# The down projection's seven products in another form, with the weights' sums made on chip ahead of their use

## The chip, the cores and the metric

The kernel runs on one core of a Trainium2 chip. The metric is the device time of one execution in microseconds (us), lower is better; the figure for a kernel is the median of several runs. Beside it stands one profiled execution, whose span runs from its first to its last instruction. The engines are named as the profile names them: PE multiplies matrices (PEld is its weight load), DVE, ACT and POOL (GpSimd) work on tiles, SP only issues transfers.

## What is computed

One step of a hybrid decoder layer over 1032 tokens (1024 of a prompt, 8 of a second group):

```python
hn = rmsnorm(x, norm1_w)
...
x = x + jnp.concatenate([y_ssd, y_pool], axis=-1) @ w_out
hn = rmsnorm(x, norm2_w)
...
u, ffn_new = causal_dwconv(u, ffn_buf, ffn_conv_w, ffn_conv_b)
...
x = x + (jax.nn.silu(gate) * val) @ w_down
```

and a last RMS norm. The first product with `w_out` is the output projection; the last, with the 2816 x 1024 matrix `w_down`, the down projection. Everything is in float32.

## The kernel before, in words

**Arithmetic.** A float32 product is made of three matmuls in a reduced format: each operand is split into a high part (an ACT copy) and a low part (a DVE subtraction of the high part from the value), and high x high, high x low and low x high are added up in PSUM. `split` (L207) does this for moving operands, `weight_parts` (L132 to 142) for weights. Weights come from DRAM into a `raw` tile (a pool of four) or an `s` tile (a pool of seven), and their two parts lie in one `wop` tile (a pool of four). So each transfer of weights waits for the split of an earlier block, and each split for PE to be done with an earlier `wop`.

**Stages.** After the state-space and pooling parts comes the output projection (`w_out`, L896): its operands `yh`, `yl` are split six at a time, and each of the eight output tiles takes 6 + 6 + 4 of them. Beside it `down_sums` (L1240) makes sums of blocks of `w_down` for later: twelve calls, each with four SP loads, four GpSimd additions or subtractions (L1253) and four GpSimd stores to DRAM scratch (L1255). Then the up projection runs over 22 pairs of 128-wide tiles of the feed-forward width (`up_pair`); `up_close` (L1184) does the convolution, SiLU and gate, and `spill` (L1226) writes what the down projection will need to DRAM scratch `td`: for each two tiles of the width, seven rows of 128 x 516, one row for each of seven products.

**The down projection** (`down`, L1305) is one 2 x 2 step of fast matrix multiplication: the width is cut into even and odd tiles (11 each), the tokens into halves of 516, the outputs into four pairs of tiles. Seven block products take the place of eight. For each product, `down_ops` (L1262) loads eleven 128 x 516 operands from `td` through GpSimd's queue (L1270, `g<-td`) and splits them; `down_weights` (L1277) loads 12 weight pieces (four output pairs m by three groups of 4, 4 and 3 width tiles); `piece` (L1291) issues 18 or 24 matmuls of 128 x 258 for a piece, the two quarters of tokens one after the other; and a `sink` adds the result into `x2`, the running sum of the layer, or, in before, into `u`. In all 7 x 264 = 1848 matmuls. The order of products before is p1, p2, p5, p6, p7, p4, p3. In p1, p2 and p4 the weights are single blocks of `w_down`; the other four read their sums back from scratch (`s<-sd`). The first product runs its pieces over all four m for one group of width tiles before the next group, in all eight PSUM banks; the others finish an m before they start the next. Squares for the last norm are made by ACT and added up by GpSimd (L1367) as blocks of `x2` are finished, and `norm_half` (L1459) writes the first half of the tokens out.

**What sets the order.** The code states what depends on what. The order of the instructions on each engine is fixed when the kernel is built, by a scheduler that goes by its own estimate of when each could start; at run time each engine takes its instructions strictly in that order and waits at each for what it needs. Issuing a transfer on GpSimd's queue is such an instruction: a transfer stands behind any addition written before it.

Of the kernel before, what the change touches and what calls it, by code (L numbers as in the profile page):

```python
# [75 lines left out]
class Kernel:  # L76
# [817 lines left out]
    def w_out(self, pf):  # L894
# [12 lines left out]
        self.sums = {}  # L907
        todo = [(m, s) for s in range(len(PIECES)) for m in range(KT // 2)]

        def part(ops, k0, first, done=None):  # L910
            for n in range(KT):
                if first <= n < first + 6:
                    self.down_sums(len(todo), *todo.pop(0))
# [9 lines left out]
                if done is not None:  # L923
                    done(n)

        part(ops, 0, 0)
# [5 lines left out]
        part(ops, 6, 1)  # L932
# [251 lines left out]
    def up_close(self, j, us):  # L1184
# [4 lines left out]
        if j == FT - 1:  # L1189
            self.begun = self.down_ops("p1", 0, 4)  # L1190
            high = self.high
# [32 lines left out]
    def spill(self, x, y, s, t):  # L1224


        nc = self.nc
        a, b = slice(0, TH), slice(TH, TOK)
        td = self.dram.tile([7, P, TH], F32, name=self.nm("td"))
        self.td.append(td)  # L1230
        rows = lambda r, n: td[r : r + n].rearrange("s p c -> p s c")
        halves = lambda t: t[:, :TOK].rearrange("p (s c) -> p s c", s=2)
        for out, in0, in1 in (
            (s[:, a], x[:, b], x[:, a]), (s[:, b], y[:, b], x[:, b]),
            (t[:, a], y[:, b], s[:, a]), (t[:, b], y[:, a], t[:, a]),
        ):
            nc.vector.tensor_tensor(out=out, in0=in0, in1=in1, op=ALU.subtract)
        self.puts += [(td[0], x[:, a]), (rows(1, 2), halves(y)), (rows(3, 2), halves(s)), (rows(5, 2), halves(t))]

    def down_sums(self, i, m, s):  # L1240

        nc, d = self.nc, self.d
        k0, nk = PIECES[s]
        w = nk * P
        mk = lambda tag, bufs=1: self.ph.tile([P, 2, 512], F32, tag=tag, name=self.nm("ds"), bufs=bufs)
        x, y, z = mk("v", 2), mk(("mh", "ml")[i % 2]), mk(("sa", "sb")[i % 2])
        blk = {"11": x[:, 0, :w], "12": x[:, 1, :w], "21": y[:, 0, :w], "22": y[:, 1, :w]}
        for k, r, e in (("21", 1, 0), ("22", 1, 1), ("11", 0, 0), ("12", 0, 1)):
            o = (e * DK + k0) * P
            nc.sync.dma_start(blk[k], d["wdn"][2 * m + r][:, o : o + w])  # L1250

        def mix(p, out, in0, in1, op):
            nc.gpsimd.tensor_tensor(out=out, in0=in0, in1=in1, op=op)  # L1253
            self.sums[p, m, s] = self.dram.tile([P, w], F32, name=self.nm("sd"))
            nc.gpsimd.dma_start(self.sums[p, m, s], out)  # L1255

        s2 = z[:, 0, :w]
        mix("p5", blk["22"], blk["21"], blk["22"], ALU.add)
        mix("p7", blk["21"], blk["11"], blk["21"], ALU.subtract)
        mix("p6", s2, blk["22"], blk["11"], ALU.subtract)  # L1260
        mix("p3", blk["12"], blk["12"], s2, ALU.subtract)
# [15 lines left out]
    def down_weights(self, p, m, s, pool=None):  # L1277

        k0, nk = PIECES[s]
        w = nk * P  # L1280
        if p in DIRECT:
            i, e = DIRECT[p]
            o = (e * DK + k0) * P
            src = self.d["wdn"][2 * m + i][:, o : o + w]
        else:
            src = self.sums[p, m, s]
        raw = self.raw(p not in DIRECT)[:, :w]
        self.nc.sync.dma_start(raw, src)
        return self.weight_parts(raw, w, self.nc.vector, pool)

    def piece(self, out, both, ops, s, q):  # L1291

        nc = self.nc
        k0, nk = PIECES[s]
        part = slice(q * TQ, (q + 1) * TQ)
        for i in range(nk):
            wh, wl = both[:, i * P : (i + 1) * P], both[:, 512 + i * P : 512 + (i + 1) * P]
            xh, xl = (t[:, part] for t in ops[k0 + i])
            for j, (a, b) in enumerate(((wh, xh), (wh, xl), (wl, xh))):
                self.pe = nc.tensor.matmul(  # L1300
                    out, a, b, start=(s == 0 and i == 0 and j == 0),
                    stop=(s == len(PIECES) - 1 and i == nk - 1 and j == 2),
                ).ins

    def down(self, ops):  # L1305
# [19 lines left out]
        us = [self.big.tile([P, 2, TH], F32, tag="big", name=self.nm("U")) for _ in range(2)]  # L1325

        def sink(p, m, q, ps):
            part = slice(q * TQ, (q + 1) * TQ)
            u = us[m // 2][:, m % 2, part]
            block = lambda i, t: x2[2 * m + i][:, half(t)][:, part]  # L1330

            def add(eng, out, in1):
                eng.tensor_tensor(out=out, in0=out, in1=in1, op=ALU.add)  # L1333

            if p == "p1":
                nc.scalar.activation(u, ps, AF.Copy)  # L1336
            elif p == "p2":
                add(nc.vector, block(0, 0), u)
                add(nc.vector, block(0, 0), ps)
            elif p == "p5":  # L1340
                add(nc.vector, block(0, 1), ps)
                add(nc.vector, block(1, 1), ps)
# [270 lines left out]
```

## Time and profile before

| | |
|---|---|
| median of 3 runs | 1409.72 us |
| lowest, highest | 1406.89, 1411.45 us |
| the profiled execution | 1407.76 us |
| its span | 1406.0 us |
| mean granted clock of PE in it | 0.984 |

An instruction's row gives its engine, the line of the kernel, the operation, the tile that it writes and those that it reads, their shapes and how many instructions the row holds. A group's row gives the busy time of all and the mean of one in ns, then the idle time just before them on their engine and what ended most of it. A row of the timeline starts with its start and length. The granted clock of a window is 1.00 when PE has its full clock.

### The profile page before, as it was taken

The page shows a single profiled execution, that of the slowest core. Times are in us where ns is not written, and L with a number is a line of the kernel's source. Part 1 is how long each engine was busy: PE and PEld are TensorE (multiplying, and loading weights), DVE is VectorE, ACT ScalarE, POOL GpSimd, SP SyncE. Part 2 cuts the span into 40 slices and gives each one's busy share as a digit, 9 for nine tenths or more (in the row PEclk, how much of TensorE's full clock was granted, in tenths as well). Part 3 has the DMA queues.
Part 4 walks back from the last instruction along what each step waited for, and adds up shares of the span by engine and source line. Part 5 has one row for each costly group of instructions (what it writes and reads, how often), then busy time and mean ns, then how long its engine had stood idle before and what let it go on. Part 6 is the DMA issues. An engine that isn't in the chain of part 4 may idle for free. (4 is left out here: it accounts for less than half of the span.)

```text
span 1406.0 us, 26779 instructions
## 1 busy us (share of the span) xinstructions
PE 1360.4 (97%) x10360; PEld 1312.9 (93%) x10360; DVE 991.2 (70%) x1453; ACT 700.6 (50%) x1408; POOL 561.5 (40%) x704
## 2 busy tenths in 40 slices
PE   8999999979999999999979999999999999999997
PEld 7799879968799999899979999999999999999997
DVE  6575898669865684844689877777776787567743
ACT  6346774546644451311456545554554465444452
POOL 4233465888668305774222212212222224214122
PEclk9999999989999999999999999999999999999999
DMA  6031235243331256675477877777777769657513
GB/s 248 1 108 38 93 118 168 81 142 116 94 104 62 74 192 209 214 253 178 152 204 148 210 205 193 187 207 183 185 187 201 196 207 328 225 185 235 180 55 121
DMA packets 117820, 228.09 MB, mean 162 GB/s; under 512 B 19884, under 2 KB 37116, under 8 KB 117692
## 3 DMA queue, kind: packets, MB, share of 16 engines
q1 hardware_dynamic: 73772, 130.21, 29.3%
q0 software_dynamic: 27056, 70.22, 19.8%
q10 hardware_dynamic: 16864, 25.95, 5.6%
q8 instruction: 81, 1.33, 0.4%
q14 instruction: 47, 0.39, 0.1%
HBM read 169.64 MB, written 45.15 MB: 153 GB/s over the span
## 5 line engine op out<-in xcount | busy, mean ns | idle before, releaser
L1118 PE MATMUL g<-op,wop 128*128 128x258 f32 x3696 | 446.9, 283 | 4.3 <-DVE op L1048 1.6
L1118 PEld LDWEIGHTS g<-op,wop 128*128 128x128 f32 x3696 | 445.3, 189 | 5.6 <-DVE op L1048 2.0
L140 ACT ACTIVATE wop<-raw 128x512 fp32r<-128x512 f32 (+1 forms) x208 | 125.9, 608 | 231.2 <-PE g L161 139.7
L1300 PE MATMUL g<-op,wop 128*128 128x258 f32 x1848 | 224.9, 283 | 1.6 <-ACT op L210 0.9
L159 PE MATMUL g<-hh,wop 128*128 128x344 f32 x696 | 226.1, 325 | 0.0
L160 PE MATMUL g<-hl,wop 128*128 128x344 f32 x696 | 225.3, 324 | 0.0
L1300 PEld LDWEIGHTS g<-op,wop 128*128 128x128 f32 x1848 | 222.5, 189 | 2.7 <-ACT op L210 1.1
L161 PE MATMUL g<-hh,wop 128*128 128x344 f32 x696 | 224.8, 323 | 0.0
L141 DVE TENSOR_TENSOR wop<-raw,wop 128x512 fp32r<-128x512 f32 (+1 forms) x186 | 159.7, 862 | 83.3 <-ACT wop L140 81.5
L140 ACT ACTIVATE wop<-s 128x512 fp32r<-128x512 f32 (+1 forms) x136 | 83.6, 620 | 137.6 <-PE g L1300 51.9
L1098 POOL DMA_DIRECT2D s<-s x44 | 37.7, 857 | 249.8 <-DVE wop L141 89.2
L159 PEld LDWEIGHTS g<-hh,wop 128*128 128x128 f32 x696 | 132.2, 190 | 1.2 <-issue 1.1
L161 PEld LDWEIGHTS g<-hh,wop 128*128 128x128 f32 x696 | 132.1, 190 | 1.2 <-issue 1.2
L160 PEld LDWEIGHTS g<-hl,wop 128*128 128x128 f32 x696 | 132.1, 190 | 0.5 <-issue 0.4
L1200 DVE SCALAR_TENSOR_TENSOR acc<-u,cst,acc 128x1048 f32<-128x1048 f32 x88 | 115.2, 1309 | 12.2 <-ACT acc L1198 10.6
L141 DVE TENSOR_TENSOR wop<-s,wop 128x512 fp32r<-128x512 f32 (+1 forms) x136 | 92.1, 682 | 36.5 <-ACT wop L140 34.1
L1178 DVE TENSOR_TENSOR u<-u,g 128x258 f32<-128x258 f32 (+2 forms) x176 | 58.0, 354 | 72.2 <-PE g L1118 67.6
L1175 ACT ACTIVATE u<-g 128x258 f32<-128x258 f32 (+2 forms) x220 | 69.6, 340 | 71.2 <-PE g L1118 71.2
L160 PE MATMUL g<-yl,wop 128*128 128x344 f32 x288 | 93.4, 325 | 3.2 <-DVE yl L211 3.2
L161 PE MATMUL g<-yh,wop 128*128 128x344 f32 x288 | 93.0, 323 | 0.0
L159 PE MATMUL g<-yh,wop 128*128 128x344 f32 x288 | 92.9, 323 | 0.0
L1270 POOL DMA_DIRECT2D g<-td x77 | 41.2, 539 | 123.1 <-DVE op L211 70.2
(276 smaller groups left out, 2333.9 us busy)
## 6 DMA issues: line engine op xcount, KB each, us to landing
s<-wup SPq DMA_DIRECT2D x88, 256.0 KB, 3.2
g<-td POOLq DMA_DIRECT2D x77, 258.0 KB, 4.5
raw<-wup SPq DMA_DIRECT2D x66, 256.0 KB, 4.1
raw<-win SPq DMA_DIRECT2D x58, 256.0 KB, 2.7
mix<-acd SPq DMA_DIRECT2D x16, 768.0 KB, 4.5
td<-acc ACTq DMA_DIRECT2D x22, 516.0 KB, 6.1
s<-wup POOLq DMA_DIRECT2D x44, 256.0 KB, 5.3
s<-s POOLq DMA_DIRECT2D x44, 256.0 KB, 3.9
```

The lines of the kernel that those rows point to most:

```text
L140: self.nc.scalar.activation(hi, raw[:, :w], AF.Copy)
L141: lo_eng.tensor_tensor(out=lo, in0=raw[:, :w], in1=hi.bitcast(F32), op=ALU.subtract)
L159: nc.tensor.matmul(ps[:, :n], wh, xh[:, sl], start=(first and k == 0), stop=False)
L160: nc.tensor.matmul(ps[:, :n], wh, xl[:, sl], start=False, stop=False)
L161: nc.tensor.matmul(ps[:, :n], wl, xh[:, sl], start=False, stop=(final and k == last))
L1098: nc.gpsimd.dma_start(t, raw[acc] if acc in raw else w[acc][j], accum_op=ALU.add)
L1118: nc.tensor.matmul(out, a, b, start=(p in OPENS and j == 1), stop=(j == 12), skip_group_check=True)
L1175: a = nc.scalar.activation(out, ps[:, s], AF.Copy, scale=-1.0 if p in ("p5", "p4") else 1.0)
L1178: nc.vector.tensor_tensor(out=out, in0=out, in1=ps[:, s], op=op)
L1200: nc.vector.scalar_tensor_tensor(out=acc, in0=u[:, k : k + FW], scalar=self.c("fw", 3 * n + k), in1=acc, op0=ALU.mult, op1=ALU.add)
L1270: self.loaded = self.nc.gpsimd.dma_start(st[:, j], self.td[i + j][ROW[p]]).ins
L1300: self.pe = nc.tensor.matmul(out, a, b, start=(s == 0 and i == 0 and j == 0), stop=(s == len(PIECES) - 1 and i == nk - 1 and j == 2),).ins
```

## The change

The seven products take another form. Their names are now n1 to n7, in the order n4, n2, n1, n5, n7, n3, n6. Two of them (n4, n3) use single blocks of `w_down`; the other five use a sum or difference of two blocks. Nothing of that is made ahead: `down_weights` loads the one block into an `s` tile and the other into a `raw` tile, and GpSimd adds them in the `s` tile before the split. That is 60 additions (40 of 128 x 512, 20 of 128 x 384) and 60 more loads than a single block would take. `down_sums` is gone, and with it everything beside the output projection. `spill` makes five sums for each two tiles rather than four, and the row of `td` that n4 reads is written first. Results go straight from PSUM into one or two blocks of `x2` (`into`), 96 additions of 128 x 258 rather than 88, with no copy to `u`. The 16 half tiles of `x2` are loaded 8 in n4, 4 in n2 and 4 in n1 (before: 4 in p1, 12 in p2). Squares are made in n2, n7, n3 and n6; `norm_half` for the first half moves from the last product into n3. In the last product the even and odd outputs change places.

```diff
-DOWN = ("p1", "p2", "p5", "p6", "p7", "p4", "p3")
-DIRECT = {"p1": (0, 0), "p2": (0, 1), "p4": (1, 1)}
-ROW = {"p1": 0, "p2": 1, "p3": 2, "p5": 3, "p7": 4, "p6": 5, "p4": 6}
+DOWN = ("n4", "n2", "n1", "n5", "n7", "n3", "n6")
+ROW = {"n2": 0, "n7": 1, "n5": 2, "n3": 3, "n6": 4, "n4": 5, "n1": 6}
+SRC = {
+    "n1": ((0, 0), (1, 1), ALU.subtract), "n2": ((1, 0), (1, 1), ALU.add), "n3": ((0, 0), None, None),
+    "n4": ((1, 1), None, None), "n5": ((0, 0), (0, 1), ALU.add), "n6": ((1, 0), (0, 0), ALU.add),
+    "n7": ((0, 1), (1, 1), ALU.add),
+}
+INTO = {
+    "n1": ((0, 0, ALU.add), (1, 1, ALU.subtract)), "n2": ((1, 0, ALU.add), (1, 1, ALU.subtract)),
+    "n3": ((0, 1, ALU.add), (1, 1, ALU.subtract)), "n4": ((1, 0, ALU.add), (0, 0, ALU.subtract)),
+    "n5": ((0, 0, ALU.subtract), (0, 1, ALU.add)), "n6": ((1, 1, ALU.add),), "n7": ((0, 0, ALU.add),),
+}
...
-                if first <= n < first + 6:
-                    self.down_sums(len(todo), *todo.pop(0))
...
-        for out, in0, in1 in (
-            (s[:, a], x[:, b], x[:, a]), (s[:, b], y[:, b], x[:, b]),
-            (t[:, a], y[:, b], s[:, a]), (t[:, b], y[:, a], t[:, a]),
+        for out, in0, in1, op in (
+            (t[:, a], y[:, a], x[:, a], ALU.subtract), (t[:, b], x[:, a], y[:, b], ALU.add),
+            (s[:, a], x[:, b], y[:, b], ALU.subtract), (s[:, b], x[:, a], x[:, b], ALU.add),
+            (y[:, a], y[:, a], y[:, b], ALU.add),
         ):
...
-        self.puts += [(td[0], x[:, a]), (rows(1, 2), halves(y)), (rows(3, 2), halves(s)), (rows(5, 2), halves(t))]
+        self.puts += [(rows(5, 2), halves(t)), (td[0], x[:, a]), (rows(3, 2), halves(s)), (rows(1, 2), halves(y))]
...
-        raw = self.raw(p not in DIRECT)[:, :w]
-        self.nc.sync.dma_start(raw, src)
-        return self.weight_parts(raw, w, self.nc.vector, pool)
+        one, two, op = SRC[p]
+        raw = self.raw(two is not None)[:, :w]
+        nc.sync.dma_start(raw, block(*one))
+        if two is not None:
+            more = self.raw(False)[:, :w]
+            nc.sync.dma_start(more, block(*two))
+            nc.gpsimd.tensor_tensor(out=raw, in0=raw, in1=more, op=op)
+        return self.weight_parts(raw, w, nc.vector, pool)
...
+    def into(self, x2, p, m, q, ps):
+
+        ins = None
+        for i, t, op in INTO[p]:
+            out = x2[2 * m + i][:, t * TH + q * TQ : t * TH + (q + 1) * TQ]
+            ins = self.nc.vector.tensor_tensor(out=out, in0=out, in1=ps, op=op).ins
+        return ins
...
-        ops += self.down_ops("p1", len(ops), DK - 1)
-        second = self.down_ops("p2", 0, 8)
-        ops += self.down_ops("p1", DK - 1)
+        ops += self.down_ops("n4", len(ops), DK - 1)
+        second = self.down_ops("n2", 0, 8)
+        ops += self.down_ops("n4", DK - 1)
...
+        whole = {"n2": (1, 0), "n7": (0, 0), "n3": (0, 1)}
...
-                load_x2([(n, 0) for n in range(0, KT, 2)])
+                load_x2([(n, 0) for n in range(KT)])
...
+                if p in whole:
+                    i, t = whole[p]
+                    square(2 * m + i, t)
+                if p == "n3" and m == 1:
+                    with self.behind(self.pe):
+                        self.norm_half(x2, 0, ssq[0], r_of(0))
```

The order of GpSimd's instructions at the end of the first product, before. Rows of `g` load operands two to a tile: here six of p2's and then p1's last one, `g_13225`; the `x` row loads half a tile of `x2`.

```order
L1270 DMA g_13198<-td_8997 128x516
L1270 DMA g_13198<-td_9514 128x516
L1270 DMA g_13207<-td_10031 128x516
L1270 DMA g_13207<-td_10548 128x516
L1270 DMA g_13216<-td_11065 128x516
L1270 DMA g_13216<-td_11582 128x516
L1270 DMA g_13225<-td_13151 128x516
L1322 DMA x_13234<-x2d 128x516
```

The same place now; `g_13008` is n4's last operand, the `s` rows are sums of n2's weights, each of an `s` tile and a `raw` tile.

```order
L1271 TENSOR_TENSOR s_13399<-s_13399,raw_13401 128x512
L1271 TENSOR_TENSOR s_13431<-s_13431,raw_13433 128x512
L1271 TENSOR_TENSOR s_13463<-s_13463,raw_13465 128x384
L1252 DMA g_12990<-td_9807 128x516
L1252 DMA g_12990<-td_10325 128x516
L1271 TENSOR_TENSOR s_13496<-s_13496,raw_13498 128x512
L1271 TENSOR_TENSOR s_13528<-s_13528,raw_13530 128x512
L1271 TENSOR_TENSOR s_13560<-s_13560,raw_13562 128x384
L1271 TENSOR_TENSOR s_13595<-s_13595,raw_13597 128x512
L1252 DMA g_12999<-td_10843 128x516
L1252 DMA g_12999<-td_11361 128x516
L1252 DMA g_13008<-td_12933 128x516
```

Seven sums now stand between the operand loads and ahead of the first product's last one.

SP's queue at the same place, before: the last four weight pieces of p1, then the first four of p2.

```order
L1288 DMA raw_13482<-wdn 128x384
L1288 DMA raw_13507<-wdn 128x384
L1288 DMA raw_13532<-wdn 128x384
L1288 DMA raw_13557<-wdn 128x384
L1288 DMA raw_13614<-wdn 128x512
L1288 DMA raw_13643<-wdn 128x512
L1288 DMA raw_13672<-wdn 128x384
L1288 DMA raw_13701<-wdn 128x512
```

And now: the last four pieces of n4 (L1267), then second blocks for n2's sums (L1270), whose first blocks have been issued earlier.

```order
L1267 DMA raw_13271<-wdn 128x384
L1267 DMA raw_13298<-wdn 128x384
L1267 DMA raw_13325<-wdn 128x384
L1267 DMA raw_13352<-wdn 128x384
L1270 DMA raw_13401<-wdn 128x512
L1270 DMA raw_13433<-wdn 128x512
L1270 DMA raw_13465<-wdn 128x384
L1270 DMA raw_13498<-wdn 128x512
```

The tiles `raw_13401` and on take the buffers of the pieces above them, as p2's blocks did before, and GpSimd's sums now read them.

GpSimd's queue in the third product, before: the operand loads of p5 in one run, its last one `g_14005`.

```order
L1270 DMA g_13978<-td_10031 128x516
L1270 DMA g_13978<-td_10548 128x516
L1270 DMA g_13987<-td_11065 128x516
L1270 DMA g_13987<-td_11582 128x516
L1270 DMA g_13996<-td_12099 128x516
L1270 DMA g_13996<-td_12616 128x516
L1270 DMA g_14005<-td_13151 128x516
```

And now, those of n1, its last one `g_13836`; the `ssq` row adds up squares of n2's results, `s_14281` is a sum for the next product.

```order
L1328 TENSOR_TENSOR ssq_13013<-ssq_13013,sq_13788 128x516
L1271 TENSOR_TENSOR s_14167<-s_14167,raw_14169 128x512
L1252 DMA g_13818<-td_10843 128x516
L1252 DMA g_13818<-td_11361 128x516
L1271 TENSOR_TENSOR s_14199<-s_14199,raw_14201 128x384
L1271 TENSOR_TENSOR s_14281<-s_14281,raw_14283 128x512
L1252 DMA g_13827<-td_11879 128x516
L1252 DMA g_13827<-td_12397 128x516
L1252 DMA g_13836<-td_12933 128x516
```

Sums of n1's own weights and of n5's first piece now lie between n1's operand loads.

More of the change, by code (lines that the diff above doesn't have):

```diff
@@ L905, in w_out, with part @@
             self.x2.append(t)
-        self.sums = {}
-        todo = [(m, s) for s in range(len(PIECES)) for m in range(KT // 2)]
-        def part(ops, k0, first, done=None):
+        def part(ops, k0):
             for n in range(KT):
-                if first <= n < first + 6:
-                    self.down_sums(len(todo), *todo.pop(0))
                 nk = len(ops)
@@ L922, in part @@
                 (self.gemm_k if n == KT - 1 else self.gemm)(ws, ops, evac)
-                if done is not None:
-                    done(n)
-        part(ops, 0, 0)
+        part(ops, 0)
         ops = []
@@ L931, in w_out @@
             ops.append(o)
-        part(ops, 6, 1)
+        part(ops, 6)
         ops = []
@@ L1324, in down @@
         half = lambda t: slice(t * TH, (t + 1) * TH)
[L1325 to L1342, printed above, removed]
-            elif p == "p6":
-                add(nc.vector, u, ps)
-                add(nc.vector, block(0, 1), u)
-            elif p == "p7":
-                add(nc.vector, u, ps)
-                add(nc.vector, block(1, 1), u)
-            elif p == "p4":
-                add(nc.vector, block(1, 0), u)
-                add(nc.vector, block(1, 0), ps)
-            else:
-                add(nc.vector, block(0, 1), ps)
+        cut = lambda ops, s: ops[PIECES[s][0] : PIECES[s][0] + PIECES[s][1]]
         mksq = lambda: self.ph.tile([P, TH], F32, tag="sq", name=self.nm("sq"), bufs=2)
@@ L1434, in down @@
                     ones()
-                if q == 0 and m == 1:
-                    with self.behind(self.pe):
-                        self.norm_half(x2, 0, ssq[0], r_of(0))
             ones()
```

89 lines of the change are left out of this document (31 added, 58 removed).

## The prediction

> **What bounds the kernel now.** I began with the page: span, engine shares, slices; then the chain of waits for the down projection; then windows over the stages that the change touches.
>
> ```profile
> span 1406.0 us, 26779 instructions
> PE 1360.4 (97%) x10360; PEld 1312.9 (93%) x10360; DVE 991.2 (70%) x1453; ACT 700.6 (50%) x1408; POOL 561.5 (40%) x704
> 1170.50 27.88 PE g L1300 x233
> ...
> 1200.34 6.10 DMA raw<-wdn
> ...
> 1207.75 155.47 PE g L1300 x1297
> ```
>
> PE is busy for 97%. In the down projection the chain is one run of 1297 matmuls, 155.47/1297 = 0.120 us each, behind one wait for a weight block, so a product of 264 matmuls takes 31.7 us. Both kernels do 7 x 264 = 1848 of them, so only what makes PE wait or run slow counts. The windows (length; busy time and instructions of PE, weight load, DVE, ACT, POOL; granted clock; DMA share; GB/s) show where it does:
>
> ```profile
> 560.00:580.00 20.00, 20.00 (x129) 20.00 (x128) 14.81 (x13) 4.05 (x7) 15.35 (x17) 1.00 0.82 273
> 580.00:600.00 20.00, 16.82 (x89) 16.09 (x88) 19.90 (x15) 7.97 (x10) 14.46 (x14) 0.83 0.55 170
> 585.00:590.00 5.00, 2.40 (x16) 2.12 (x14) 5.00 (x1) 0.97 (x2) 4.98 (x6) 0.96 0.37 138
> 590.00:595.00 5.00, 4.41 (x14) 3.97 (x15) 5.00 (x8) 3.38 (x4) 0.09 (x1) 0.50 0.80 249
> 595.00:600.00 5.00, 5.00 (x29) 5.00 (x28) 5.00 (x5) 0.53 (x1) 4.39 (x4) 0.85 0.59 135
> 1200.00:1210.00 10.00, 9.10 (x75) 8.85 (x74) 7.06 (x15) 5.42 (x13) 2.14 (x4) 1.00 0.93 346
> 1210.00:1360.00 150.00, 150.00 (x1256) 150.00 (x1255) 98.55 (x185) 70.75 (x128) 34.51 (x53) 1.00 0.52 166
> 1360.00:1370.00 10.00, 9.27 (x70) 8.68 (x70) 5.96 (x11) 7.07 (x16) 2.55 (x2) 1.00 0.19 62
> ```
>
> From 1210 to 1360 PE never idles, DVE has 98.55 of 150 us and GpSimd 34.51. The output projection loses time at 585 to 595, and there GpSimd is adding.
>
> **The change, part by part.** *A, the output projection.* Rows of the timelines of DVE, GpSimd and PE (start, length, instruction):
>
> ```profile
> 578.19 11.96 DVE L211 TENSOR_TENSOR yl<-xs,yh 128x1032 fp32r<-128x1032 f32 x4
> 590.54 1.22 DVE L211 TENSOR_TENSOR yl<-xs,yh 128x1032 fp32r<-128x1032 f32 x1
> 579.17 4.54 POOL L1253 TENSOR_TENSOR ds<-ds,ds 128x512 f32<-128x512 f32 x2
> 537.30 0.51 DVE L920 TENSOR_TENSOR x<-x,g 128x344 f32<-128x344 f32 x1 [0.57 <-PE g L161]
> 590.21 0.66 PE L160 MATMUL g<-yl,wop 128*128 128x344 f32 x1 [2.80 <-DVE yl L211]
> ```
>
> One subtraction alone takes 1.22 us; four beside GpSimd's adds (two of them at 579.17) take 11.96 instead of 4.9. PE waits 2.80 us for the last, then runs at a clock of 0.50. The window from 580 holds 89 matmuls and the one before it 129, 0.155 us each, so 40 are missing: 40 x 0.155 = 6.2 us. The change takes the adds away: **-6.2** (-6.2 to 0: zero if the split is late for another reason).
>
> *B, the first product's last operand.* The groups and transfers that price the new work (count, busy time, mean ns; a transfer's last figure is us from issue to landing):
>
> ```profile
> L1253 POOL TENSOR_TENSOR ds<-ds,ds 128x512 f32<-128x512 f32 x24 | 33.3, 1409 | 3.0 <-DMA ds<-wdn 2.8
> L1253 POOL TENSOR_TENSOR ds<-ds,ds 128x384 f32<-128x384 f32 x12 | 12.4, 1043 | 3.9 <-DMA ds<-wdn 3.8
> L1270 POOL DMA_DIRECT2D g<-td x77 | 41.2, 539 | 123.1 <-DVE op L211 70.2 <-PE g L1300 20.6 <-PE g L1118 13.2
> L210 ACT ACTIVATE op<-g 128x516 fp32r<-128x516 f32 x77 | 45.6, 622 | 3.3 <-DMA g<-td 2.1 <-DVE acc L1237 1.0
> g<-td POOLq DMA_DIRECT2D x77, 258.0 KB, 4.5
> raw<-wdn SPq DMA_DIRECT2D x24, 256.0 KB, 4.4
> s<-sd SPq DMA_DIRECT2D x32, 256.0 KB, 2.9
> raw<-wdn SPq DMA_DIRECT2D x8, 256.0 KB, 6.0
> x<-x2d POOLq DMA_DIRECT2D x16, 258.0 KB, 7.4
> ```
>
> The last two are of 1165 to 1205 alone. Before, the first product's last operand load leaves at 1172.44; it needs only an early tile. Now GpSimd's row of n4's last operand stands behind seven sums of n2 and four operand loads. The sums need second blocks, which SP loads into the four `raw` tiles, and those come free only as n4's pieces 9 to 12 are split. Before, the same tiles came free for p2's first four loads at these times:
>
> ```profile
> 1172.44 0.54 POOL L1270 DMA_DIRECT2D g<-td  x1 [5.86 <-DVE wop L141]
> 1187.33 0.87 SPq L1288 DMA_DIRECT2D raw<-wdn  x2
> 1189.83 0.33 SPq L1288 DMA_DIRECT2D raw<-wdn  x1
> 1192.68 0.33 SPq L1288 DMA_DIRECT2D raw<-wdn  x1
> ```
>
> With 4.4 us to land, sum 1 starts at 1191.8 and sums 1 to 3 end at 1193.2, 1194.6, 1195.7; two operand loads go until 1196.8. Sum 4 waits for the block of 1192.68, lands 1197.1, ends 1198.5. Sums 5 to 7 use the tiles that sums 1 to 3 freed, end at 1199.9, 1200.9, 1202.4. Two loads more, then the last operand's leaves at 1203.5, lands 4.5 later at 1208.0, and its high part is there 0.62 later: 1208.7. PE's order puts the 24 matmuls that use it at n4's end; p1's ended at 1198.39 by the chain, so PE is dry at 1198.39 - 24 x 0.12 = 1195.5. Wait: **+13.2** (9.9 with 2.9 to land, 16.8 with 6.0). Behind it on GpSimd stand n4's eight loads of x2, without which its sums can't leave PSUM: first issues 1204.1 and 1204.7, 7.4 to land, 1212.1, against n4's end at 1208.7 + 2.9: **+1** (0 to 4).
>
> *C, the clock after that wait.* By the rows above 2.80 us of idling were followed by a clock of 0.50 for about 6 us, a loss of 3.0: **+3.0** (0 to 3). The Trainium skill, "TensorE: Matmul & The Clock Gate", Part 1, has the clock halved after an idle window of about 3.4 us and back after about as long of activity. The first the row contradicts (2.80 us did it); by the second a wait costs about 1.7, and the sum would be 1.6 lower over this wait and D's.
>
> *D, n1.* Between n2's last operand and n1's last, GpSimd has 14 sums, 3 adds of squares and 15 loads, some 30 us for a product of 31.7, and it is tied to PE. n1's k8 load stands behind a sum of n5 whose `s` tile comes free when n1's sixth piece is split, for which PE must be 48 matmuls (5.8 us) into n1. Then, by the rows above and below, split 0.63 + 0.70, load of a block 2.9, sum 1.41, issue 0.54, landing 4.5, high part 0.62: 17.1 us after n1's start. PE gets to k8 after 96 matmuls, 11.5 us, and is 5.6 us early. k6, behind a sum whose tile n2's end frees, is there at about 13 and wanted after 72 matmuls, 8.6: 4.4 of the 5.6 fall there, 1.2 at k8. One add of squares in between (1.3) makes it **+7** (4 with 2.9 to land and no squares; 13 with the block landing in 6.0 and the operand in 7.4), and a second wait's clock **+2** (0 to 3).
>
> *E, n2, n5, n7, n6.* In n5 the k10 load stands behind a sum of n7; by steps like D's the operand is there 17.3 us into the product, wanted after 141 matmuls, 16.9. The last loads of n2, n7 and n6 stand behind sums in the same way. I choose about 1 each: **+4** (0 to 16, each wait like D's 4.4 at k6, less a little).
>
> *F.* Two gaps of before, 0.90 us at 1200 to 1210 and 0.73 at 1360 to 1370, need not come back: **-1** (-1.6 to 0).
>
> *At no cost.* Eleven more spill additions, one for each pair of up-projection tiles, like these:
>
> ```profile
> L1237 DVE TENSOR_TENSOR u<-acc,u 128x516 f32<-128x516 f32 x11 | 7.6, 690 | 0.0
> ```
>
> They run on DVE beside PE's matmuls of the up stage (7.6 us if that cover were gone). Eight more DVE adds of 0.42 into x2, hidden while DVE has a third free, 3.4 otherwise. Sixty more SP loads, 0.33 of issue each; their 40 x 256 + 20 x 192 KB over the 220 us of the projection are 64 GB/s, beside 166 at a DMA share of 0.52. The ACT copies of p1's results go, off the path. The norm of the first half moves a product earlier and runs beside matmuls either way.
>
> **Sum.** -6.2 + 13.2 + 1 + 3 + 7 + 2 + 4 - 1 = +23.0. On the profiled execution's 1407.8 us that is 1430.8. The median of the runs, 1409.7, lies 2.0 above it: **1433 us**. The lower ends give 1416, the upper 1466.
>
> **Rivals.**
>
> *Lock bound, 1424.* GpSimd's adds and DVE's operations on two operands in SBUF exclude each other:
>
> ```profile
> L211 DVE TENSOR_TENSOR op<-g,op 128x516 fp32r<-128x516 f32 x77 | 53.9, 721 | 3.0 <-ACT op L210 2.9
> L141 DVE TENSOR_TENSOR wop<-s,wop 128x512 fp32r<-128x512 f32 x120 | 83.6, 699 | 23.2 <-ACT wop L140 20.8
> L141 DVE TENSOR_TENSOR wop<-s,wop 128x384 fp32r<-128x384 f32 x16 | 8.9, 554 | 13.3 <-ACT wop L140 13.3
> L140 ACT ACTIVATE wop<-s 128x512 fp32r<-128x512 f32 x120 | 75.6, 633 | 117.5 <-PE g L1118 49.1 <-issue 36.2 <-PE g L1300 32.2
> L1333 DVE TENSOR_TENSOR x<-x,g 128x258 f32<-128x258 f32 x40 | 15.8, 419 | 23.7 <-PE g L1300 23.7
> L1367 POOL TENSOR_TENSOR ssq<-ssq,sq 128x516 f32<-128x516 f32 x10 | 13.2, 1331 | 32.3 <-ACT sq L1366 25.6 <-ACT ssq L1363 6.5
> ```
>
> A product takes DVE 11 x 0.721 + 8 x 0.699 + 4 x 0.554 = 15.7, and GpSimd's sums 8 x 1.409 + 4 x 1.043 = 15.4: 31.1 of 31.7 if exclusive. In n2 and n7, 4 x 1.331 of squares make it 36.4, 4.7 over each. If operand loads are not held otherwise: 1407.8 - 6.2 - 1 + 9.4 + 2 = 1412; where the adds from PSUM cannot overlap either (16 x 0.42 = 6.7, half in n7 and n6), up to 1437. Middle 1424. For it: A's 11.96 us. Against its upper end: the PSUM add at 537.30 took 0.51 beside an add of GpSimd. The Trainium skill, "SBUF — State Buffer", "SBUF: two separate sides", states this as a lock on a port pair that the two engines share, for the whole instruction; 11.96 us for four agrees. Chance 0.12.
>
> *Cascade, 1456.* Each sum waits for a `raw` tile, each tile for an earlier sum, and GpSimd's row is in order, so lateness in n1 is handed on: n2, n5 and n7 lose 6.5 each instead of 3 of E's 4 together (+16.5), and two more waits are long enough to halve the clock (+6): 1433 + 22.5. It decides if GpSimd's 30 us of work per product can't start before the product. Chance 0.20.
>
> *Faster, 1402.* The other side: n4's last operand leaves 13.2 us sooner than I have it, by 1190.3, because the `raw` tiles come free earlier than before's; no later wait opens. Then only A and F stay: 1407.8 + 2.0 - 6.2 - 1.6. Against it: the times above are set by PE's pace through pieces 5 to 8, which the change leaves. Chance 0.06.
>
> *The output projection doesn't gain, 1439.* The split could be late because its inputs are. The four subtractions ran end to end with GpSimd's adds, so I give this 0.06, inside my forecast's range.
>
> **How the numbers follow.** Forecast 0.52 beside the last rival's 0.06, which lies within 1420 to 1445 too; lock bound 0.12, cascade 0.20, faster 0.06; 0.04 stays for sums that cancel to within 0.3%, 4.2 us, about what a measurement here tells from no change. Faster 0.06, same 0.04, slower 0.90. The range runs from the lock rival's lower end, taken as 1413, to just above the cascade, 1460; outside lie the faster case, most of the same and the cascade's upper third.
>
> **What would show it.** Right: DVE's four yl subtractions at about 4.9 us and no clock of 0.50 near 590; a wait of PE of some 13 us for n4's last operand with GpSimd's adds of line 1271 ahead of its load; a shorter pair of waits about 8 to 12 us into n1; half clock behind each. Wrong: no PE wait at n4's end (then B, C fall, and it is near 1413 or below); waits of PE on DVE's splits rather than on operand loads (lock); waits above 4 us in n5 and n7 (cascade).

## The result and the profile after

The changed kernel takes 1453.7 us (median of 4 runs, 1450.7 to 1456.3), the kernel before beside it 1408.3: a ratio of 1.0323, 95% interval 1.0285 to 1.0362, or 45 us more. The forecast of 1433 was 21 us short; the range, 1413 to 1460, holds it.

The page of the changed kernel has these first lines:

```profile
span 1449.8 us, 26760 instructions
PE 1370.5 (95%) x10360; PEld 1318.3 (91%) x10360; DVE 1010.8 (70%) x1472; ACT 700.6 (48%) x1400; POOL 552.1 (38%) x668
```

PE does the same matmuls and now idles 79 us, before 46. Of the 44 us that the span grew, 34 are idle time of PE; the other 10 are the same matmuls taking longer, at a mean granted clock of 0.976 instead of 0.984. No other engine has come near to its limit, and GpSimd is, over the whole span, even less busy than before. So it is waiting, and a lower clock, and not work, that has been added. The windows of the changed kernel at the places that the prediction named (columns as before):

```profile
580.00:600.00 20.00, 20.00 (x129) 20.00 (x129) 12.52 (x19) 6.02 (x9) 0.00 (x0) 1.00 0.16 46
1198.00:1205.00 7.00, 6.66 (x37) 6.66 (x38) 5.12 (x13) 2.72 (x5) 1.65 (x4) 0.62 0.88 331
1210.00:1350.00 140.00, 125.93 (x994) 122.84 (x993) 102.76 (x141) 53.29 (x95) 84.20 (x95) 0.96 0.73 241
```

The output projection now does 129 matmuls from 580 to 600 at full clock, and DVE's four subtractions take 4.94 us instead of 11.96:

```profile
574.52 4.94 DVE L222 TENSOR_TENSOR yl<-xs,yh 128x1032 fp32r<-128x1032 f32 x4
```

From 1210 to 1350 PE loses 14 us, where the kernel before lost none from 1210 to 1360. Where PE waits is read from its timeline; the last bracket gives the wait and what ended it:

```profile
1160.82 26.78 PE L1283 MATMUL g<-op,wop 128*128 128x258 f32 x223
1198.34 37.36 PE L1283 MATMUL g<-op,wop 128*128 128x258 f32 x292 [10.75 <-ACT op L221]
...
1253.49 28.49 PE L1283 MATMUL g<-op,wop 128*128 128x258 f32 x219 [4.41 <-ACT op L221]
...
1382.10 7.44 PE L1283 MATMUL g<-op,wop 128*128 128x258 f32 x60 [2.44 <-DVE wop L152]
1395.18 4.54 PE L1283 MATMUL g<-op,wop 128*128 128x258 f32 x18 [5.64 <-ACT wop L151]
1404.02 0.58 PE L1283 MATMUL g<-op,wop 128*128 128x258 f32 x1 [4.30 <-ACT op L221]
...
1407.86 4.59 PE L1283 MATMUL g<-op,wop 128*128 128x258 f32 x21 [1.94 <-ACT wop L151]
```

The trace also gives the length of each product: the matmuls of the down projection are counted by their single records, and a product ends where each 264th ends. This table has the lengths in us, for the two kernels and for experiments told below. The first product is counted from the projection's first matmul.

| kernel | 1st | 2nd | 3rd | 4th | 5th | 6th | 7th | all |
|---|---|---|---|---|---|---|---|---|
| before | 34.6 | 32.9 | 31.5 | 31.6 | 31.6 | 31.6 | 36.7 | 230.6 |
| changed | 47.7 | 31.6 | 43.5 | 37.7 | 35.0 | 35.3 | 52.4 | 283.2 |
| no sums (e1) | 34.5 | 32.5 | 31.7 | 31.5 | 31.6 | 32.9 | 40.8 | 235.5 |
| narrow sums (e2) | 47.3 | 31.7 | 37.5 | 38.0 | 38.5 | 32.5 | 46.3 | 271.8 |
| sums by DVE (e4) | 49.4 | 32.0 | 39.8 | 36.5 | 31.6 | 32.6 | 46.5 | 268.3 |
| n2's sums later (e5) | 34.8 | 33.1 | 44.6 | 39.2 | 34.2 | 38.8 | 53.6 | 278.5 |
| last product single (e7) | 48.0 | 32.2 | 44.4 | 38.5 | 34.4 | 32.8 | 41.8 | 272.1 |
| sums of one block (e9) | 34.5 | 32.5 | 39.1 | 34.4 | 33.8 | 33.8 | 47.7 | 255.8 |
| narrow, one block (e12) | 34.5 | 32.5 | 32.2 | 36.0 | 31.5 | 32.7 | 42.8 | 242.3 |

The projection became 52.6 us longer: 13.1 in n4, 12.0 in n1, 6.1 in n5, 3.4 in n7, 3.7 in n3 and 15.7 in n6, while n2 takes 1.3 less than p2.

The chain of waits shows two of these. At n4's end:

```profile
1179.53 2.91 DMA raw<-wdn
...
1182.47 2.27 POOL s L1271 x2
...
1188.49 1.21 POOL s L1271
...
1192.06 1.08 POOL g L1252 x2
1193.14 4.49 DMA g<-td
...
1198.34 5.69 PE g L1283 x27
```

Read upwards: PE waits for an operand, whose load left late, behind sums on GpSimd, which waited for second blocks. In n1:

```profile
1239.22 4.84 DMA s<-wdn
...
1244.19 1.19 POOL s L1271
...
1245.69 1.52 POOL ssq L1328
...
1247.40 1.54 POOL s L1271
1248.94 3.84 DMA g<-td
...
1253.49 2.52 PE g L1283 x10
```

A load of a first block, a sum, an addition of squares, another sum, and only then the operand that PE needs.

In n6 all of the loss lies in the first half: its 132 matmuls take 34.7 us (1386.5 to 1421.2), in the kernel before 19.0. PE waits there before the 25th (5.64) and before the 43rd to 46th matmul (4.30 and less). From 1395 to 1412 the granted clock is 0.51, and after that PE waits no more, though weight pieces are still to come. The first wait follows a split on DVE, with additions of GpSimd beside it; the second is again for an operand whose load stood behind a sum that waited for a second block:

```profile
1388.49 4.46 DVE L152 TENSOR_TENSOR wop<-s,wop 128x384 fp32r<-128x384 f32 x1
1389.07 1.01 POOL L1271 TENSOR_TENSOR s<-s,raw 128x384 f32<-128x384 f32 x1
1390.03 1.27 POOL L1328 TENSOR_TENSOR ssq<-ssq,sq 128x516 f32<-128x516 f32 x1
1391.26 1.26 POOL L1271 TENSOR_TENSOR s<-s,raw 128x512 f32<-128x512 f32 x1
```

```profile
1396.32 2.78 DMA raw<-wdn
...
1399.27 0.43 POOL s L1271
...
1400.20 3.11 DMA g<-td
```

That one split took 4.46 us, where the mean of such splits in the kernel before is 0.55. Behind it stood additions into `x2` in DVE's row, and behind these in ACT's row a square and the high part of the weights for which PE waited.

### The profile page after: what moved, and what is told of

Same layout as the page of the kernel before. It is cut to its first block, busy times and chain, and to the rows that moved or that the text cites. A ratio compares the mean times of both kernels' runs of the same rounds, so it can differ in the third digit from the quotient of the medians.

```text
span 1449.8 us, 26760 instructions
## 1 busy us (share of the span) xinstructions
PE 1370.5 (95%) x10360; PEld 1318.3 (91%) x10360; DVE 1010.8 (70%) x1472; ACT 700.6 (48%) x1400; POOL 552.1 (38%) x668
## 4 chain that ended last, share of the span: by engine, by line
PE 72%; DVE 10%; DMA 8%; POOL 4%; issue 4%; ACT 2%; DVEq 0%; SPq 0%; POOLq 0%; ACTq 0%
PE g L1122 29%; PE g L171 10%; PE g L170 10%; PE g L172 10%; PE g L1283 8%; DVE wop L152 2%; DMA g<-td 2%; DVE op L222 1%; DMA s<-wdn 1%; DVE x L1292 1%; PE pY L631 1%; POOL s L1271 1%; DMA mix<-acd 1%; DMA raw<-wdn 1%; PE pY L641 1%
## 5 line engine op out<-in xcount | busy, mean ns | idle before, releaser
L1122 PE MATMUL g<-op,wop 128*128 128x258 f32 x3696 | 448.7, 284 | 3.4 <-ACT op L1047 3.2
L1122 PEld LDWEIGHTS g<-op,wop 128*128 128x128 f32 x3696 | 447.6, 191 | 4.2 <-ACT op L1047 3.6
L1283 PE MATMUL g<-op,wop 128*128 128x258 f32 x1848 | 239.5, 291 | 39.6 <-ACT op L221 20.7
L1283 PEld LDWEIGHTS g<-op,wop 128*128 128x128 f32 x1848 | 232.7, 196 | 45.2 <-ACT op L221 21.8
L151 ACT ACTIVATE wop<-raw 128x512 fp32r<-128x512 f32 (+1 forms) x196 | 118.7, 608 | 199.7 <-PE g L172 142.3
L152 DVE TENSOR_TENSOR wop<-raw,wop 128x512 fp32r<-128x512 f32 (+1 forms) x174 | 131.4, 758 | 78.3 <-ACT wop L151 77.5
L151 ACT ACTIVATE wop<-s 128x512 fp32r<-128x512 f32 (+1 forms) x148 | 89.8, 616 | 141.4 <-issue 45.3
L152 DVE TENSOR_TENSOR wop<-s,wop 128x512 fp32r<-128x512 f32 (+1 forms) x148 | 121.0, 829 | 19.2 <-ACT wop L151 17.0
L1102 POOL DMA_DIRECT2D s<-s x44 | 37.7, 858 | 245.8 <-DVE wop L152 94.5
L1271 POOL TENSOR_TENSOR s<-s,raw 128x512 f32<-128x512 f32 (+1 forms) x60 | 78.8, 1325 | 107.3 <-DMA raw<-wdn 45.4
L222 DVE TENSOR_TENSOR op<-g,op 128x516 fp32r<-128x516 f32 x77 | 69.4, 918 | 44.9 <-ACT op L221 44.8
L172 PE MATMUL g<-yh,wop 128*128 128x344 f32 x288 | 92.1, 320 | 0.0
```

Source lines behind the costliest of these rows:

```text
L151: self.nc.scalar.activation(hi, raw[:, :w], AF.Copy)
L152: lo_eng.tensor_tensor(out=lo, in0=raw[:, :w], in1=hi.bitcast(F32), op=ALU.subtract)
L172: nc.tensor.matmul(ps[:, :n], wl, xh[:, sl], start=False, stop=(final and k == last))
L222: (lo_eng or nc.vector).tensor_tensor(out=lo, in0=src, in1=hi.bitcast(F32), op=ALU.subtract)
L1122: nc.tensor.matmul(out, a, b, start=(p in OPENS and j == 1), stop=(j == 12), skip_group_check=True)
L1271: nc.gpsimd.tensor_tensor(out=raw, in0=raw, in1=more, op=op)
```

## The experiments

Theories at the start: the *queue* theory (operand loads stand behind sums in GpSimd's row) and the *lock* theory (GpSimd's additions stop DVE's splits). Ratios are to the kernel before, run on the same chip beside each group of experiments, with 95% intervals.

**e1, no sums.**

```diff
-        if two is not None:
-            more = self.raw(False)[:, :w]
-            nc.sync.dma_start(more, block(*two))
-            nc.gpsimd.tensor_tensor(out=raw, in0=raw, in1=more, op=op)
```

> The changed kernel with the second block of each weight pair and its addition left out, so the five products use single blocks (the sums of w_down are not computed); every weight still goes through an s tile. Queue theory (PE waits for operand loads that stand behind GpSimd's sums, and for the sums' own blocks): all waits of the down projection go and only the gain of the output projection is left, 1408.3 - 6.2 = about 1402, between 1397 and 1405. Lock theory (GpSimd's additions stop DVE's splits): the same. Rival that the form itself costs something (x2 loaded later, a later spill for the first product): over 1408, with a wait left at n4's end.

Measured: 1406.4 us, ratio 0.9997 (0.9961 to 1.0033). The loss against the kernel before is gone with the sums and their loads: 1453.7 - 1406.4 = 47 us (46 by the ratios). The figure lies a little above the 1397 to 1405 of both theories, and the rival's wait at n4's end is not there. The form itself gives no gain, though: the last product takes 40.8 us against 36.7. That is 4.1 of the 7.5 us that the output projection gains (e8); the rest lies within the interval. Which step of the form costs the 4.1 us is open.

**e2, narrow sums.**

```diff
-            nc.gpsimd.tensor_tensor(out=raw, in0=raw, in1=more, op=op)
+            nc.gpsimd.tensor_tensor(out=raw[:, :32], in0=raw[:, :32], in1=more[:, :32], op=op)
```

> The changed kernel with both blocks loaded and GpSimd's additions kept at their places, but each over 32 columns instead of 512 or 384 (the other columns of the sums are not computed). GpSimd's busy time for sums falls from 78.8 us to some 15 and with it what they can take from DVE; the waits for blocks and the order of its queue stay. Queue theory: most of the loss stays, 1430 to 1445. Lock theory, or GpSimd's plain busy time: 1400 to 1415.

Measured: 1441.5 us, ratio 1.0227 (1.0170 to 1.0284), 12 us below the changed kernel. Groups of the changed kernel, then the same ones of this:

```profile
L222 DVE TENSOR_TENSOR op<-g,op 128x516 fp32r<-128x516 f32 x77 | 69.4, 918 | 44.9 <-ACT op L221 44.8
L152 DVE TENSOR_TENSOR wop<-s,wop 128x384 fp32r<-128x384 f32 x20 | 22.0, 1101 | 4.9 <-ACT wop L151 4.9
L1271 POOL TENSOR_TENSOR s<-s,raw 128x512 f32<-128x512 f32 x40 | 57.4, 1442 | 93.9 <-DMA raw<-wdn 44.3 <-DMA s<-wdn 30.9 <-issue 10.2
```

```profile
L222 DVE TENSOR_TENSOR op<-g,op 128x516 fp32r<-128x516 f32 x77 | 57.6, 758 | 72.1 <-ACT op L221 71.9
L152 DVE TENSOR_TENSOR wop<-s,wop 128x384 fp32r<-128x384 f32 x20 | 11.4, 570 | 1.2 <-ACT wop L151 1.1
L1271 POOL TENSOR_TENSOR s<-s,raw 128x32 f32<-128x32 f32 x60 | 21.3, 355 | 147.4 <-DMA s<-wdn 55.6 <-DMA raw<-wdn 47.4 <-issue 19.9
```

DVE's splits are back near their lengths of before (721 and 554 ns), so the exclusion is there in the changed kernel. The Trainium skill, "SBUF — State Buffer", "SBUF: two separate sides", says that the one blocks the other for a whole instruction; splits of 1101 ns instead of 554 agree. But with the additions' own length it explains about a quarter of the loss, 12 us of 47. The sums hardly work now, yet GpSimd idles 147 us before them, 103 of it until a block lands.

**e3, operand loads from ACT's queue.**

```diff
-                self.loaded = self.nc.gpsimd.dma_start(st[:, j], self.td[i + j][ROW[p]]).ins
+                self.loaded = self.nc.scalar.dma_start(st[:, j], self.td[i + j][ROW[p]]).ins
```

> The changed kernel with the down projection's 77 operand loads issued from ACT's queue instead of GpSimd's, so that none stands behind a sum; GpSimd's additions stay at full width, and all is computed. Queue theory: the waits of ACT's high parts for operand loads (72.9 us of them in the changed kernel) and PE's 20.7 us for them go; what is left is the wait for sums in the last product, 1412 to 1425. Lock theory: DVE's splits stay as slow, 1440 or more.

Measured: 1452.7 us, ratio 1.0317 (1.0270 to 1.0365). The time is the one given for the lock theory, but neither expectation can be read from it: the loads came under another in-order row. PE's largest waits around n4's end:

```profile
PE g L1283 <- ACT op L221: 16.8, 1, 16.8
```

n4's last operand stood in ACT's row behind high parts of n2's operands, each waiting for its own load. The experiment is inconclusive on the queue theory.

**e4, sums by DVE.**

```diff
-            nc.gpsimd.tensor_tensor(out=raw, in0=raw, in1=more, op=op)
+            nc.vector.tensor_tensor(out=raw, in0=raw, in1=more, op=op)
```

> The changed kernel with the sums made by DVE instead of GpSimd; all is computed. Sixty additions at 0.69 or 0.55 us are 39 us of DVE, 8 x 0.69 + 4 x 0.55 = 7.7 a product, so a product has 15.7 + 6.7 + 7.7 = 30.1 us of DVE work for 31.7 of PE. Queue theory and lock theory both: operand loads are free and nothing excludes, 1402 to 1415, with what is left in the last product, whose twelve sums fall into its first half. Rival that DVE becomes the bound: 1425 or more.

Measured: 1437.9 us, ratio 1.0213 (1.0163 to 1.0263). Neither theory gives this time, and the rival's figure came for another reason. Its window and PE's timeline at n4's end:

```profile
1210.00:1350.00 140.00, 131.13 (x1058) 129.08 (x1058) 108.15 (x204) 57.30 (x103) 32.81 (x52) 0.98 0.75 244
```

```profile
1206.51 8.70 PE L1283 MATMUL g<-op,wop 128*128 128x258 f32 x53 [12.96 <-DVE op L222]
```

DVE is busy for 108 of 140 us, so it is not the bound over this stretch. Operand loads are free, GpSimd excludes nothing, and PE still waits 13 us at n4's end: the last operand's *split* now stands behind seven sums in DVE's row, waiting for the same blocks. The wait goes with the sums to whichever engine makes them.

That suggested two theories more. *Placement*: it is enough to put the sums behind what PE needs next. *Supply*: the sums can't be made in time wherever they stand.

**e5, n2's sums behind n4's last operand load.**

```diff
+        self.last4 = self.loaded
...
-            nc.gpsimd.tensor_tensor(out=raw, in0=raw, in1=more, op=op)
+            with self.behind(self.last4 if p == "n2" else None):
+                nc.gpsimd.tensor_tensor(out=raw, in0=raw, in1=more, op=op)
```

> The changed kernel with n2's sums placed behind the load of n4's last operand in GpSimd's queue, and nothing else; all is computed. Placement theory (whatever PE needs next stands, in an in-order queue, behind sums that wait for blocks): PE's wait of 10.75 us at n4's end and the half clock after it, 7 us at 0.62 or 2.7 us, go: 1453.7 - 13 = about 1440. Rival, supply theory (the sums can't be made in time wherever they stand, since the blocks' tiles come free too late): the wait moves into n2, 1450 or more.

Measured: 1451.1 us, ratio 1.0287 (1.0259 to 1.0315). PE's timeline:

```profile
1196.51 31.48 PE L1284 MATMUL g<-op,wop 128*128 128x258 f32 x261 [1.29 <-DVE wop L152]
...
1244.29 7.28 PE L1284 MATMUL g<-op,wop 128*128 128x258 f32 x48 [7.92 <-ACT op L221]
```

The wait at n4's end is gone and n4 is 12.9 us shorter, but the later products took back 8.0 by the table, spread over n2, n1, n5, n3 and n6. The kernel is 3 us faster by the medians and 5 by the ratios and by the table, which is not clear of the noise. That speaks for supply, not for placement at one spot, though the wait did not move into n2 alone.

**e6, each product's sums behind its first six operand loads.** (The same `behind`, with a mark set anew in each product, the last one too.)

```diff
-                ops = self.down_ops(p)
+                ops = self.down_ops(p, 0, 6)
+                self.gate = self.loaded
+                ops += self.down_ops(p, 6)
```

> The changed kernel with each product's sums placed behind the first six operand loads of that product (n2's behind n4's last), so that fewer operand loads stand behind sums; all is computed. Placement theory: waits of n4, n1, n5 and n7 shrink, 1415 to 1432, with the last product's left. Supply theory: each product now starts with its sums to come, three to five us a product more, 1450 to 1470.

Measured: 1450.4 us, ratio 1.0288 (1.0256 to 1.0321). As supply has it: PE's waits for operands shrink and those for weights grow. Of PE's waits in the down projection, the changed kernel's first, then this one's:

```profile
PE g L1283 <- ACT op L221: 20.7, 5, 10.7
...
PE g L1283 <- DVE wop L152: 5.7, 5, 2.4
```

```profile
PE g L1284 <- DVE wop L152: 14.7, 8, 3.5
...
PE g L1284 <- ACT op L221: 7.4, 2, 5.9
```

**e7, the last product with single blocks.**

```diff
-    "n6": ((1, 0), (0, 0), ALU.add),
+    "n6": ((1, 0), None, None),
```

> The changed kernel with single blocks as the last product's weights (its twelve sums are not computed, its twelve second loads are gone). The last product uses all twelve weight pieces in its first half, 132 matmuls or 15.9 us, against 15.4 us of GpSimd for the sums alone. Theory that this rate costs the last product its extra 14 us: 1453.7 - 10 to 14, so 1440 to 1444 (the kernel without sums keeps 3.7 us of waits there). Rival that it is the first half's norm with its stores, moved next to it: 1450 or more.

Measured: 1443.1 us, ratio 1.0231 (1.0203 to 1.0260), 10.5 below the changed kernel (13 by the ratios); the last product went from 52.4 to 41.8. So twelve of the sixty sums cost some 10 to 13 us, and the norm moved next to them does not. That they cost so much because the rate of sums is too low for a product that uses all twelve pieces in its first half is argued, not shown: the trace has two waits there, told above, and none behind the 46th matmul. The rest over before's 36.7 is there without any sums too (e1, 40.8).

**e8, the kernel before without its sums.**

```diff
-                if first <= n < first + 6:
-                    self.down_sums(len(todo), *todo.pop(0))
...
-            src = self.sums[p, m, s]
+            src = self.d["wdn"][2 * m][:, k0 * P : k0 * P + w]
```

> The kernel before with the sums beside the output projection left out; the four products that read them back load single blocks of w_down instead (so their sums are not computed), at the same count of transfers. If the output projection's missing 40 matmuls are due to GpSimd's additions there: 1406.4 - 6.2 = about 1400. Rival that the time is given back behind it: 1406.

Measured: 1401.2 us, ratio 0.9947 (0.9925 to 0.9970), or -7.5 us (-10.6 to -4.2). The output projection's loss is real, is due to those sums with their loads and stores, and isn't given back.

**e9, full sums of one block.**

```diff
-            more = self.raw(False)[:, :w]
-            nc.sync.dma_start(more, block(*two))
-            nc.gpsimd.tensor_tensor(out=raw, in0=raw, in1=more, op=op)
+            nc.gpsimd.tensor_tensor(out=raw, in0=raw, in1=raw, op=op)
```

> The changed kernel with all sixty of GpSimd's additions at full width, but each of the first block with itself, so no second block is loaded (the sums of w_down are not computed). GpSimd has its 79 us of sums and DVE its contention; the second loads, their four raw tiles and the sums' waits for them are gone. Second-load theory (sums and what stands behind them wait for blocks whose tiles come free late): 1410 to 1420. Theory that a sum in GpSimd's queue is enough, whatever it waits for: 1435 or more.

Measured: 1427.6 us, ratio 1.0160 (1.0124 to 1.0196), between the two. It lies between the two expectations as well. n4's end is clean (34.5), n1 and n6 are not (39.1 and 47.7).

**e10, two tiles more for second blocks.**

```diff
-            more = self.raw(False)[:, :w]
+            self.nth = getattr(self, "nth", -1) + 1
+            more = (self.spool.tile([P, 512], F32, tag="two", name=self.nm("two"), bufs=2) if self.nth % 3 == 0 else self.raw(False))[:, :w]
```

> The changed kernel with two more tiles for second blocks: every third one gets a tile of its own pool of two, so six can be under way instead of four; all is computed. If the count of four raw tiles is what makes the blocks late: 1425 to 1440. If it is not (the s tiles, freed by DVE's splits at PE's pace, or the order of the queues set it): 1448 or more.

Measured: 1459.5 us, ratio 1.0378 (1.0346 to 1.0411). Slower: four `raw` tiles are not what is short, or two more don't mend it. SP still waits there 46 us for sums to free such tiles, as in the changed kernel. Why the run lost 6 us was not pursued.

**e11, the kernel before with its sums by DVE.**

```diff
-            nc.gpsimd.tensor_tensor(out=out, in0=in0, in1=in1, op=op)
+            nc.vector.tensor_tensor(out=out, in0=in0, in1=in1, op=op)
```

> The kernel before with the 48 sums beside the output projection made by DVE instead of GpSimd, the stores still GpSimd's; all is computed. Without two engines at it at once a sum takes DVE 0.69 or 0.55 us, 31 us in a stage where DVE has some 40% of its time free. If the output projection's loss is the exclusion of the two engines, its 6 us come back: 1400 to 1404. Rival that DVE's queue then waits for the sums' blocks ahead of PE's operands: 1406 or more.

Measured: 1402.2 us beside 1403.7 for the kernel before in its group, ratio 0.9983 (0.9961 to 1.0004): perhaps faster, not shown. The window in the output projection and the group of its subtractions, which have a mean of 1819 ns in the kernel before:

```profile
580.00:600.00 20.00, 18.77 (x119) 18.36 (x118) 19.24 (x26) 10.55 (x13) 4.86 (x9) 1.00 0.84 284
```

```profile
L211 DVE TENSOR_TENSOR yl<-xs,yh 128x1032 fp32r<-128x1032 f32 x12 | 14.5, 1228 | 1.1 <-ACT yh L210 1.1
```

The exclusion is gone (1228 ns a subtraction) and 119 matmuls fit instead of 89; the ten that still lack are 1.5 us, with DVE busy for 19.24 of 20 us.

**e12, narrow sums of one block** (what e2 and e9 change, together).

```diff
-            more = self.raw(False)[:, :w]
-            nc.sync.dma_start(more, block(*two))
-            nc.gpsimd.tensor_tensor(out=raw, in0=raw, in1=more, op=op)
+            nc.gpsimd.tensor_tensor(out=raw[:, :32], in0=raw[:, :32], in1=raw[:, :32], op=op)
```

> The changed kernel with the two cuts before put together: sixty additions by GpSimd, each over 32 columns and of the first block with itself, no second block loaded (the sums of w_down are not computed). What is left of the sums is that an operand load can stand behind an instruction that waits for an s tile's load. If the two costs add, full width 12 us and the second block 26, and the rest of the 47 us over the kernel without sums is this order: 1427.6 - 12 = 1415. If the order costs nothing by itself: 1406, as without sums. If the width costs little once no second block is awaited: 1422 or more.

Measured: 1409.7 us, ratio 1.0031 (1.0008 to 1.0054). With it there is a square of four:

| ratio to before | one block | two blocks |
|---|---|---|
| 32 columns | 1.0031 | 1.0227 |
| full width | 1.0160 | 1.0323 |

Sixty short additions in GpSimd's row cost little by themselves, 0.34% over e1, which is within the noise. The second block costs 1.96% with narrow sums and 1.63% with full ones, 23 to 28 us; the width, which is GpSimd's own time and the exclusion together, 1.29% or 0.96%, 14 to 18 us. The single differences are known to about half a per cent, and they nearly add up. So the second blocks are the larger part, and the additions' length the other.

How the second blocks cost it, the waits of SP's queue suggest. In e2, then in e12 (us in total, times, longest):

```profile
SPq L1270 <- POOL s L1271: 72.4, 41, 4.8
SPq L1267 <- DVE wop L152: 63.3, 27, 12.1
```

```profile
SPq L1267 <- DVE wop L152: 147.3, 51, 17.1
```

In e12 SP waits mainly for `s` tiles that PE's pace frees, so it is ahead. In e2 it waits 72 us for `raw` tiles that sums must free, 41 times (46 us, 31 times, in the changed kernel), and the loads of first blocks stand behind that in SP's row, while GpSimd's sums wait 55.6 us for just those. Each would then wait for the other's last step. That this circle is the cause was argued from these waits; no run took it apart. The sums' waits for first blocks prove little by themselves: in e12 they are longer, and cost next to nothing.

```profile
L1269 POOL TENSOR_TENSOR s<-s 128x32 f32<-128x32 f32 x60 | 24.4, 408 | 107.0 <-DMA s<-wdn 81.5 <-DVE wop L152 11.0 <-DVE op L222 10.3
```

Slower transfers are a rival that stays open. Between 1200 and 1400 us a first block lands after 4.4 us in e2 and after 3.2 in e12 (256 KB each), while the core's transfers move 247 and 166 GB/s; operand loads are not much slower (4.3 and 3.9):

```profile
s<-wdn SPq DMA_DIRECT2D x35, 256.0 KB, 4.4
```

```profile
s<-wdn SPq DMA_DIRECT2D x31, 256.0 KB, 3.2
```

## Why the prediction was right or wrong, point by point

- **A, right.** -6.2 forecast, -7.5 (-10.6 to -4.2) measured by e8. By the traces the cause is the one named: DVE's four subtractions take 4.94 us beside no addition. In time e11, which takes away the exclusion alone, does not show it clear of noise.
- **B and C, right in mechanism and near in size.** 13.2 forecast, 10.75 measured; the chain has it as foreseen, blocks, sums, then the operand load. Most of the difference is a misreading: 1198.39 is only where the chain left PE, and p1's 264th matmul ends at 1200.05, with which the forecast's own sum gives 11.5. The 24 matmuls behind the wait took 5.3 us instead of 2.9, so the slow clock lost 2.4 against 3.0. By the 3.4 us of the Trainium skill ("TensorE: Matmul & The Clock Gate", Part 1) it would have been about 1.7, an estimate; 2.4 was measured. The half tiles of `x2` cost nothing. Together 13.1, where B and C had 17.2. But the term was no independent one: with it taken away in e5, the kernel gained 3 to 5 us.
- **D, right in its longest wait, short in sum.** 9 forecast for n1, 12.0 measured. The chain at 1239 to 1253 has the steps of the forecast: a first block's load, sums and squares, the operand's load, its high part. PE waits 4.41 us for it before the 73rd matmul of n1, as forecast for k6 (4.4); the wait at k8 did not come. Three waits for low parts, 3.1 us together, came early in n1 and stood in no term.
- **E, the step that failed.** "I choose about 1 each: **+4**", for n2, n5, n7 and n6. The price was chosen, not worked out, and its upper end of 16 was too low as well. n5, n7, n3 and n6 lost 6.1 + 3.4 + 3.7 + 15.7 = 28.9, which is more than the whole miss of 21; n3 was in no term. The largest, 15.7 in the last product, is in part of the kind that E named, an operand load behind a sum (4.30 at the 43rd matmul), at four times the price. The rest E did not have: 5.64 behind a split that took 4.46 us beside GpSimd's additions, and a clock of 0.51 behind these waits. Of the 15.7, e7 puts 10.6 on the sums and e1 4.1 on the form.
- **Sum.** -7.5 + 13.1 - 1.3 + 12.0 + 28.9 = 45.2, the measured 45. That it meets so closely is luck, as the first term alone is known to 3 us. B and C were 4 too high and D 3 too low; the miss is E's.
- **F** came in half: n2 takes 1.3 less than p2, whose gap of 0.90 us is gone; in the last product nothing was gained.
- **At no cost**, right for the spill's additions (from 900 to 1100 PE is busy for 200 of 200 us in both kernels), wrong for the loads: sixty more cost 23 to 28 us, as waits or by slower landing.
- **The range** holds the result partly by luck: it reaches to 1460 for the cascade's sake, and what filled it is mainly the last product, to which the forecast and the cascade gave about 1.
- **Rivals.** The exclusion is there, and costs at most the 14 to 18 us of the width, not the whole. The cascade came nearest in time, 1456, though it put 6.5 each on n2, n5 and n7, where -1.3, 6.1 and 3.4 were measured, and its sign, waits above 4 us in n5 and n7, did not come. The faster case and the one without gain in the output projection are out.

## What to carry to other kernels

A step that waits for two loads, put into an in-order row, delays whatever stands behind it; giving it to another engine moved the wait there (e4), and moving one group of sums brought less than half of the 13 us that it took out of n4 (e5), so such waits are not priced one by one. Look at the stretch in which a supply is used fastest, and not only at a whole product: the last product uses its twelve weight pieces in its first half, and lost all of its 15.7 us there. Before moving work "off a busy stage", take the work out altogether (e1, e8): the two runs bounded the gain, 7.5 us, and the price, 47 us.

## What the runs showed that was not expected

A profiled execution can differ ahead of the place of the change: the projection's first matmul came at 1155.9 us in the changed kernel, 1160.0 in e5 and 1162.7 in e10, whose code ahead of it is the same. So spans of single executions tell differences of 7 us and less badly, and lengths of stages, as in the table, tell them better. In the output projection the 48 sums made by DVE (e11) left ten matmuls missing from 580 to 600, by GpSimd forty. One split of 384 columns took 4.46 us while GpSimd was adding, which the group's mean of 1101 ns does not show.
